# One small tile padded from 64 to 128 bytes, which shifts the on-chip address of every tile behind it

## The chip, the cores and the metric

The kernel runs on one core of one Trainium2 chip. The metric is the device time of one execution in microseconds (us). A core has five engines that run side by side: PE (TensorE, the matmuls; its weight loads are listed apart as PEld), DVE (VectorE), ACT (ScalarE), POOL (GpSimd) and SP (SyncE, which issues the DMAs here). The on-chip memory has 128 partitions; a tile is a rectangle of 128 partitions by some bytes, and its address is the byte within the partition at which it begins.

## The reference

One decoder block on `x` of 512 tokens by 1024 channels, all in float32:

```
h = RMSNorm(x);  [glu | q | k | v | g | gates] = h @ w_in
A: a = glu_a * sigmoid(glu_b) -> causal depthwise conv (31 taps) -> LayerNorm -> swish -> @ w_conv_proj
B: retention of 4 heads (rotary q, k; decay), norm per head, swish(g) gate -> @ w_ret_proj
x = x + (sigmoid(gA) * A + sigmoid(gB) * B) @ w_out
x = x + (silu(conv3(u1)) * conv3(u2)) @ w_down     with  [u1 | u2] = RMSNorm(x) @ w_up   (2 x 3072)
out = RMSNorm(x)
```

## The kernel before

Channels lie on the partitions and the 512 tokens along the free axis, so that an activation is a set of tiles of 128x512 float32 (2048 bytes in each partition). Every operand of a matmul is split in two rounded parts, high and low, and a product is made of three matmuls: high by high, high by low, low by high (L146 to L148 in `unit`). The part called lhsT is the stationary operand, loaded as a weight of 128x128; rhs is the moving operand, streamed column by column. In a row of the trace the moving tile stands first: `ps<-xg,whi` moves `xg` past the weights `whi`.

The weights come in one stream of 184 blocks of 128x1024 in the order of use. SP loads a block into `wraw` (3 buffers), ACT rounds it into `whi`, DVE subtracts to get `wlo` (3 buffers each, L92 to L108); this runs two blocks ahead of PE. The order of the work is fixed by the program: it is written out by hand, and a scheduler with priorities puts the long convolution on DVE (L337) behind everything else.

The stages, with the tile that moves through PE:

- Per head h = 0 to 3 (some 25 to 490 us): the projections of `h` move `xg`, the scaled input. `values` (L386) is the other way round: it moves the weights and loads `xg`. `scores` and `inner` (L416 to L455) move `A` (q, k, v), `sh` and `sl` (the scores), with 512, 384, 256 and 128 columns. `ret_proj` of the head before (L476) moves `R`.
- Gates and the last head's `ret_proj`, four times two units of `xg` and two of `R`; then the convolution's projection (L527), which moves `A` and `C` (high parts in `A`, low ones in `C`); then `w_out`, which moves `xg`.
- The feed-forward part: 48 units of `w_up` move `A`. `w_down` comes in two halves: each unit of the first moves eight `xg` tiles and four `R`, each of the second eight `xg` and four `C`. The last two units of the second half are cut in halves of 256 columns (L604 to L606) so that the final norm can begin.

Tiles of one tag lie together, and the tags follow each other in the order in which they are first used; each tile takes its own size, rounded up to 32 bytes. So the size of one tile sets the address of all tags that come after it. The tile concerned is `rtok` (L293): four float32 numbers per partition are used, the inverse norm of the tokens, written at L299 and read at L402; it is allocated as 16 numbers, 64 bytes.

Of the kernel before, what the change touches and what calls it, by code (L numbers as in the profile page):

```python
# [9 lines left out]
F32 = mybir.dt.float32  # L10
# [4 lines left out]
P = 128  # L15
# [6 lines left out]
NCH = S // P  # L22
# [25 lines left out]
def hybrid_block(  # L48
# [11 lines left out]
    sb = ctx.enter_context(tc.tile_pool(name="sb", bufs=1))  # L60
# [229 lines left out]
    with tc.high_priority(offset=-200):  # L290
        for i in range(KT):
            ss.add(xs[i])
    r_tok = sb.tile([P, 4 * NCH], F32, tag="rtok", name="rtok")[:, 0:NCH]  # L293
    rB = [None]
    cosr = sb.tile([P, S], F32, tag="cosr", name="cosr")
    sinr = sb.tile([P, S], F32, tag="sinr", name="sinr")
# [464 lines left out]
```

## Time and profile before

| | us |
|---|---|
| median of three runs (1089.64 to 1089.98) | 1089.82 |
| the profiled execution | 1090.43 |
| its span, first to last instruction | 1088.6 |
| PE busy | 1076.8 |
| DVE busy | 759.7 |
| ACT busy | 420.9 |

The profile is of one execution. Busy time of PE has overlaps in it, because each matmul begins before the one before it has ended: a matmul of 512 columns is listed with some 390 ns, but the next one begins about 227 ns after it. What counts for the time is this distance from start to start, called pitch below. It is read from the timeline as the difference of two start times, divided by the number of matmuls between them.

### The profile page before, as it was taken

To read this page: it belongs to the slowest core of one execution; us is meant where nothing else is said; L and a number is where in the kernel's file an instruction comes from. 1 tells how busy PE (TensorE), PEld (TensorE's weight loads), DVE (VectorE), ACT (ScalarE), POOL (GpSimd) and SP (SyncE) were. 2 spreads that over 40 slices of the span, in tenths; PEclk is the share of its full clock that TensorE was granted. 3 is DMA by queue.
4 is the path that set the end of the run, shared out by engine and by line. 5 is a ranking of instruction groups with operands and counts; after the bars stand their busy time and mean duration, and the time that the engine had idled before them with its cause. 6 is when DMAs were issued, how large, how long until landed. Compare 5 with 4: busy or idle time off the path is not lost.

```text
span 1088.6 us, 12567 instructions
## 1 busy us (share of the span) xinstructions
PE 1076.8 (99%) x4946; PEld 896.5 (82%) x4946; DVE 759.7 (70%) x1070; ACT 420.9 (39%) x555; POOL 20.0 (2%) x72
## 2 busy tenths in 40 slices
PE   8999999999999999999999999999999999999997
PEld 7888888888888888888888888888888888888886
DVE  5999699739996599937664555577777335767433
ACT  6343333434233331534462334444444113444331
POOL 1000000000000000000000000000000000000000
PEclk9999999999999999999999999999999999999999
DMA  7222132313222122222222432232222222222212
GB/s 273 97 97 87 59 97 97 101 64 97 96 97 88 58 97 97 80 76 78 97 97 97 145 126 97 78 110 95 93 95 95 96 96 97 97 97 97 97 58 78
DMA packets 32475, 105.48 MB, mean 97 GB/s; under 512 B 3616, under 2 KB 5920, under 8 KB 32416
## 3 DMA queue, kind: packets, MB, share of 16 engines
q1 hardware_dynamic: 32416, 104.69, 28.9%
q8 instruction: 38, 0.62, 0.2%
q14 instruction: 21, 0.17, 0.1%
HBM read 102.58 MB, written 2.10 MB: 96 GB/s over the span
## 4 chain that ended last, share of the span: by engine, by line
PE 97%; issue 1%; DVE 1%; DMA 0%; SPq 0%; ACT 0%; POOLq 0%; POOL 0%; DVEq 0%
PE ps L146 28%; PE ps L148 27%; PE ps L147 27%; PE ps L395 3%; PE ps L393 3%; PE ps L394 3%; PE ps L452 1%; PE ps L451 1%; PE ps L450 1%; PE ps L221 1%; PE ps L190 1%; PE ps L427 0%; PE ps L429 0%; PE ps L425 0%; DMA wraw<-in_wst_dram 0%
## 5 line engine op out<-in xcount | busy, mean ns | idle before, releaser
L105 ACT CAST whi<-wraw 128x1024 fp32r<-128x1024 f32 (+1 forms) x185 | 193.7, 1047 | 420.7 <-PE ps L147 282.5
L106 DVE TENSOR_TENSOR wlo<-wraw,whi 128x1024 fp32r<-128x1024 f32 (+1 forms) x185 | 224.8, 1216 | 69.4 <-ACT whi L105 66.5
L146 PE MATMUL ps<-xg,whi 128*128 128x512 f32 x672 | 263.4, 392 | 0.0
L148 PE MATMUL ps<-xg,wlo 128*128 128x512 f32 x672 | 261.9, 390 | 0.0
L147 PE MATMUL ps<-xg,whi 128*128 128x512 f32 x672 | 261.6, 389 | 0.0
L146 PE MATMUL ps<-A,whi 128*128 128x512 f32 x448 | 176.3, 393 | 0.0
L148 PE MATMUL ps<-A,wlo 128*128 128x512 f32 x448 | 174.8, 390 | 0.0
L337 DVE SCALAR_TENSOR_TENSOR C<-ap,par,C 128x512 f32<-128x512 f32 x240 | 166.1, 743 | 3.1 <-ACT C L334 2.7
L147 PE MATMUL ps<-A,whi 128*128 128x512 f32 x384 | 150.2, 391 | 0.0
L148 PEld LDWEIGHTS ps<-xg,wlo 128*128 128x128 f32 x672 | 126.1, 188 | 27.0
L147 PEld LDWEIGHTS ps<-xg,whi 128*128 128x128 f32 x672 | 126.2, 188 | 26.0
L146 PEld LDWEIGHTS ps<-xg,whi 128*128 128x128 f32 x672 | 126.2, 188 | 25.6
L148 PEld LDWEIGHTS ps<-A,wlo 128*128 128x128 f32 x448 | 84.1, 188 | 19.3
L146 PEld LDWEIGHTS ps<-A,whi 128*128 128x128 f32 x448 | 84.2, 188 | 18.0
L147 PEld LDWEIGHTS ps<-A,whi 128*128 128x128 f32 x384 | 72.2, 188 | 15.1
L308 DVE TENSOR_TENSOR t<-ps,rB 128x512 f32<-128x512 f32 x48 | 32.4, 686 | 72.2 <-PE ps L148 72.2
L558 DVE SCALAR_TENSOR_TENSOR t<-ap,par,t 128x512 f32<-128x512 f32 x96 | 71.5, 748 | 1.6
L182 DVE TENSOR_TENSOR x<-x,ps 128x512 f32<-128x512 f32 (+1 forms) x50 | 33.0, 664 | 53.9 <-PE ps L148 50.4
L552 DVE TENSOR_TENSOR ap<-ps,rB 128x512 f32<-128x512 f32 x48 | 32.9, 688 | 44.4 <-PE ps L148 44.4
L146 PE MATMUL ps<-R,whi 128*128 128x512 f32 x160 | 63.1, 395 | 0.0
L148 PE MATMUL ps<-R,wlo 128*128 128x512 f32 x160 | 62.7, 392 | 0.0
L147 PE MATMUL ps<-R,whi 128*128 128x512 f32 x160 | 62.2, 389 | 0.0
(135 smaller groups left out, 1180.6 us busy)
## 6 DMA issues: line engine op xcount, KB each, us to landing
wraw<-in_wst_dram SPq DMA_DIRECT2D x183, 512.0 KB, 3.3
x<-in_xT_dram SPq DMA_DIRECT2D x16, 256.0 KB, 2.8
out_dram<-t SPq DMA_DIRECT2D x8, 256.0 KB, 2.2
dec<-in_decay_dram SPq DMA_DIRECT2D x4, 256.0 KB, 2.6
t<-in_cs_dram SPq DMA_DIRECT2D x2, 256.0 KB, 4.2
wraw<-in_wst_dram SPq DMA_DIRECT2D x1, 384.0 KB, 4.8
par<-in_params_dram SPq DMA_DIRECT2D x1, 264.0 KB, 5.3
wraw<-in_wst_dram SPq DMA_DIRECT2D x1, 128.0 KB, 2.6
```

The costliest lines, as they stand in the source:

```text
L105: nc.scalar.copy(out=hi[:, sl], in_=raw[:, sl])
L106: nc.vector.tensor_tensor(out=lo[:, sl], in0=raw[:, sl], in1=f32(hi[:, sl]), op=ALU.subtract)
L146: nc.tensor.matmul(ps, lhsT=wh, rhs=xh, start=kt == 0, stop=False)
L147: nc.tensor.matmul(ps, lhsT=wh, rhs=xl, start=False, stop=False)
L148: nc.tensor.matmul(ps, lhsT=wl, rhs=xh, start=False, stop=kt == last)
L182: nc.vector.tensor_tensor(out=acc, in0=acc, in1=v, op=ALU.add)
L337: nc.vector.scalar_tensor_tensor(out=acc, in0=a[:, k:k + S], scalar=wcol(k), in1=acc, op0=ALU.mult, op1=ALU.add)
L393: nc.tensor.matmul(banks[c], lhsT=xh[:, sl], rhs=wh, start=kt == 0, stop=False)
L394: nc.tensor.matmul(banks[c], lhsT=xl[:, sl], rhs=wh, start=False, stop=False)
L395: nc.tensor.matmul(banks[c], lhsT=xh[:, sl], rhs=wl, start=False, stop=kt == KT - 1)
L552: nc.vector.tensor_tensor(out=u[:, FK - 1:], in0=ps, in1=rB[0], op=ALU.mult)
L558: nc.vector.scalar_tensor_tensor(out=c, in0=u[:, k:k + S], scalar=wcol(k), in1=c, op0=ALU.mult, op1=ALU.add)
```

## The change

`rtok` is allocated with 32 numbers (128 bytes) in place of 16 (64 bytes); the same four are used. No instruction is added, removed or moved: on every engine the same instructions stand in the same order. What differs is the address of the tags behind `rtok`, all 64 bytes further on.

```
-    r_tok = sb.tile([P, 4 * NCH], F32, tag="rtok", name="rtok")[:, 0:NCH]
+    r_tok = sb.tile([P, 8 * NCH], F32, tag="rtok", name="rtok")[:, 0:NCH]
```

First byte of a tag in the partition, from the program as built:

| tag (buffers x bytes) | before | after | before, past a multiple of 128 / 256 / 512 | after |
|---|---|---|---|---|
| x, wraw, xg, whi, wlo, ss, t | 19456 (x), 49152 (xg), 81920 (whi), 94208 (wlo) | the same | 0 / 0 / 0 | 0 / 0 / 0 |
| rtok | 126976 | 126976 | 0 / 0 / 0 | 0 / 0 / 0 |
| cosr, sinr (1 x 2048 each) | 127040, 129088 | 127104, 129152 | 64 / 64 / 64 | 0 / 128 / 128 |
| rB (1 x 2048) | 131264 | 131328 | 64 / 192 / 192 | 0 / 0 / 256 |
| ap (3 x 2168) | 133312 | 133376 | 64 (first) | 0 (first) |
| C (8 x 2048) | 139840 | 139904 | 64 / 64 / 64 | 0 / 128 / 128 |
| dec, A (1 and 16 x 2048) | 156224, 158272 | 156288, 158336 | 64 / 64 / 64 | 0 / 128 / 128 |
| sh, sl (5120 each) | 191296, 196416 | 191360, 196480 | 64 / 64 / 320 | 0 / 128 / 384 |
| G, nB, R (4, 1 and 8 x 2048) | 201536, 209728, 211776 | 201600, 209792, 211840 | 64 / 64 / 320 | 0 / 128 / 384 |

## Rows read from the trace of the kernel before

**Rows 1.** The page: busy time by engine, and the granted clock in 40 slices.
```profile
PE 1076.8 (99%) x4946; PEld 896.5 (82%) x4946; DVE 759.7 (70%) x1070; ACT 420.9 (39%) x555; POOL 20.0 (2%) x72
PEclk9999999999999999999999999999999999999999
```
**Rows 2.** The page: the chain that ended last, shares of the span by engine.
```profile
PE 97%; issue 1%; DVE 1%; DMA 0%; SPq 0%; ACT 0%; POOLq 0%; POOL 0%; DVEq 0%
```
**Rows 3.** All waits of PE: us in total, times, longest us.
```profile
PE ps L159 <- ACT xg L176: 1.7, 1, 1.7
...
PE ps L160 <- DVE xg L177: 0.9, 2, 0.6
```
**Rows 4.** The longest wait of ACT, same columns.
```profile
ACT whi L105 <- PE ps L147: 282.5, 127, 5.6
```
**Rows 5.** Timeline of PE, stage of w_out: start us, us listed, instruction.
```profile
642.25 0.39 PE L146 MATMUL ps<-xg,whi 128*128 128x512 f32 x1
...
676.25 0.39 PE L146 MATMUL ps<-xg,whi 128*128 128x512 f32 x1
```
**Rows 6.** Timeline of PE, stage of w_up.
```profile
760.45 0.39 PE L146 MATMUL ps<-A,whi 128*128 128x512 f32 x1
...
799.59 0.39 PE L146 MATMUL ps<-A,whi 128*128 128x512 f32 x1
```
**Rows 7.** Windows inside both: us, PE busy (count), granted clock, DMA share, GB/s.
```profile
642.30:676.30 34.00, 34.00 (x152) 1.00 0.27 93
760.50:799.50 39.00, 39.00 (x172) 1.00 0.29 95
```
**Rows 8.** Matmuls by moving tile, xg: count, duration in ns min/median/max, first and last start.
```profile
L146 PE MATMUL ps<-xg,whi x672: 387/389/486, 20.4 to 1059.3; 128*128 128x512 f32 x168
...
L393 PE MATMUL ps<-whi,xg x128: 389/389/398, 54.1 to 442.7; 128*128 128x512 f32 x128
```
**Rows 9.** The same for A (L148 has as many as L146).
```profile
L146 PE MATMUL ps<-A,whi x448: 392/394/477, 591.4 to 1009.8; 128*128 128x512 f32 x150
...
L147 PE MATMUL ps<-A,whi x384: 388/394/398, 679.2 to 1010.0; 128*128 128x512 f32 x192
```
**Rows 10.** The same for R (L147 and L148 have as many).
```profile
L146 PE MATMUL ps<-R,whi x160: 392/394/443, 154.6 to 899.9; 128*128 128x512 f32 x160
```
**Rows 11.** The same for C (L148 has as many as L146).
```profile
L147 PE MATMUL ps<-C,whi x88: 388/388/397, 591.7 to 1054.0; 128*128 128x512 f32 x88
...
L146 PE MATMUL ps<-C,whi x24: 394/394/398, 1010.5 to 1053.8; 128*128 128x512 f32 x24
```
**Rows 12.** Timeline of PE, one unit of w_down, from R to xg and back.
```profile
867.59 0.40 PE L146 MATMUL ps<-xg,whi 128*128 128x512 f32 x1
...
869.90 0.39 PE L147 MATMUL ps<-xg,whi 128*128 128x512 f32 x1
...
873.08 0.40 PE L146 MATMUL ps<-R,whi 128*128 128x512 f32 x1
...
873.78 0.39 PE L146 MATMUL ps<-R,whi 128*128 128x512 f32 x1
```
**Rows 13.** Timeline of PE, head 0, from a projection into values.
```profile
53.43 0.39 PE L146 MATMUL ps<-xg,whi 128*128 128x512 f32 x1
...
54.11 0.39 PE L393 MATMUL ps<-whi,xg 128*128 128x512 f32 x1
...
54.79 0.39 PE L393 MATMUL ps<-whi,xg 128*128 128x512 f32 x1
```
**Rows 14.** Groups by line, shapes apart: 256 columns, C and xg (x, busy us, mean ns).
```profile
L605 PE MATMUL ps<-xg,whi 128*128 128x256 f32 x32 | 9.1, 283 | 0.0
...
L605 PE MATMUL ps<-C,whi 128*128 128x256 f32 x16 | 4.5, 279 | 0.0
```
**Rows 15.** Groups by line: DVE's subtraction into xg and into A.
```profile
L170 DVE TENSOR_TENSOR xg<-t,xg 128x512 fp32r<-128x512 f32 x24 | 16.5, 689 | 9.6 <-ACT xg L169 9.6
...
L170 DVE TENSOR_TENSOR A<-t,A 128x512 fp32r<-128x512 f32 x16 | 10.9, 682 | 0.0
```

## The prediction

> **What bounds the kernel now.** [...] The waits of PE come third, to see whether PE ever stands still for somebody: the longest of its five is 1.7 us, the shortest 0.9 us, and their lines (L159 to L161, L253, L221, L190) are those of the first 20 us and of the end [rows 3]. In between it goes from matmul to matmul without a pause. So no wait can be removed here, and no engine beside PE can give time back; what is left is how long one matmul keeps the next one back.
>
> That is not in the durations but in the start times, and there the trace shows two levels. In the stage of w_out, which moves `xg`, the start goes from 642.25 to 676.25 us [rows 5]. The window between holds 152 matmuls [rows 7], of which two had begun before it, so the pitch is 34.00 us / 150 = 226.7 ns. In the stage of w_up, which moves `A`, it is 760.45 to 799.59 us [rows 6] over 172 less the one that lies before the first row [rows 7]: 39.14 us / 171 = 228.9 ns. Same shape, same weights buffers, same clock, similar DMA share (0.27 and 0.29). The listed medians split in the same way: 389 ns for L146 with `xg` and for L393, which moves `whi` [rows 8], 394 ns for L146 with `A`, `R` or `C` [rows 9 to 11]. The split follows the address: `xg`, `whi` and `wlo` begin at multiples of 128 bytes, `A`, `R`, `C`, `sh` and `sl` 64 bytes past one. It doesn't follow the buffer's tag (three tags are slow alike), or the stage (w_down has both in one unit).
>
> **What the change costs and gives.** It adds and removes no instruction, and the queues keep their order, so there is no wait to be added and none to be removed. It moves the five slow tags to multiples of 128 bytes. If these set the pitch, they fall to the pitch of `xg`.
>
> First term, the steady pitch. Moving operands of 512 columns from moved tiles: 448 + 448 + 384 of `A` [rows 9], 3 x 160 of `R` [rows 10], 88 + 24 + 24 of `C` [rows 11], 1896 in all. Each is worth 228.9 - 226.7 = 2.2 ns, which is 4.2 us. Scores and inner have 18 more per head of 512 columns from `A`, `sh` and `sl` (6 and 12), 72 in all: 0.16 us.
>
> Second term, the passage between the two levels. In w_down a unit goes from `R` to `xg` and back. The first ten matmuls after the passage into `xg` take 867.59 to 869.90 us, 2.31 us where ten steady ones take 2.27: some 0.045 us lost [rows 12]. The first three after the passage into `R` take 0.70 us where three steady ones take 0.687: some 0.015 us [rows 12]. By the order of the units there are 22 passages of the first kind (3 after `ret_proj`, 4 in the gates, 1 into w_out, 8 and 6 in w_down) and as many of the second. That makes 1.0 + 0.3 = 1.3 us. It goes only if the passage between addresses is its cause and not the change of tile as such. The trace says the former: from a projection into `values`, where the moving tile changes from `xg` to `whi` and both lie on multiples of 128, three matmuls take 0.68 us before and 0.68 us behind the border [rows 13], with nothing lost.
>
> Third, the shapes that have no clean pair of rows. At 256 columns L605 is listed with 283 ns from `xg` and with 279 ns from `C` [rows 14], so the sign may turn there: 48 matmuls of the last units may lose up to 4 ns each, 0.2 us. Of the 216 narrower ones in scores and inner I know only that the wide ones differ by 2.2 ns; either way that is at most 0.5 us. I take zero for both and keep -0.5 to +0.7 us for the range.
>
> Fourth, the other engines. DVE and ACT read and write the moved tiles too. DVE's subtraction takes 689 ns into `xg` and 682 ns into `A` [rows 15], the slower one on the multiple of 128; so moving `A` may lengthen such an operation by 7 ns or shorten it. On some 600 DVE operations on moved tiles that is 4 us of 759.7 us busy, and PE is the cover: what DVE and ACT owe PE is the next weights, and ACT's longest wait is for PE to give back a `whi` buffer, 282.5 us over 127 times [rows 4], so the weights are there long before PE wants them. If this cover were gone, those 4 us would be the price. I take nothing. The DMA into a moved tile (`dec`, four times) is far ahead of its use: nothing.
>
> The sum is 4.2 + 0.2 + 1.3 = 5.7 us. The profiled execution took 1090.43 us, 1.8 us outside its span; less 5.7 that is 1084.7 us. The median of the runs is 0.6 us below the profiled one, so I forecast 1084.1 us for a median. It goes faster by 0.5%, and PE stays the bound; no other wait comes late next.
>
> [...]
>
> **The rivals.**
> No change, 1089.8 us: the offset within 128 bytes isn't what counts. Two readings of the table of addresses allow it. All slow tags lie above byte 127,000 and all fast ones below 107,000, and the change moves none across; or the step that counts is 256 bytes or more, and the moved tiles still stand 128 past a multiple of 256, while every fast one stands on a multiple of 2048. The trace can't separate these from my reading. For it: nothing that moves through PE lies high and on a multiple of 128. [...]
>
> Slower, about 1095.5 us: the excess grows with the distance from a multiple of 256. Then 64 bytes cost 2.2 ns, 128 bytes cost 4.4, and the first two terms come once more on top: 1089.8 + 5.7. [...] Against it: `R` stands 320 past a multiple of 512 and `A` 64, and both have 394 ns in L146 [rows 9, 10], so at least by 512 distance doesn't count. It decides if L146 with `A` goes above 394 ns.
>
> Half of it, 1085.5 to 1088.8 us: only the steady term goes and the passages stay (1089.8 - 4.4 = 1085.4), or only those tiles gain that also changed their place to 256 in a favourable way, or the narrow shapes lose the 0.7 us. Against it stand the rows of the border without loss.
>
> **How the numbers follow.** The forecast has 0.70, the half case 0.08, no change 0.12, slower 0.10. The forecast's own range is 1083.0 to 1085.3: the third item's bounds and half a us for the passages, of which I saw one unit. To leave out no more than 2 in 10 the range has to take in the half case and come to the edge of no change: 1082.8 to 1089.9. What a measurement can tell from no change is about 0.2%, 2.2 us. Faster by more than that is the forecast and three quarters of the half case, 0.76; the rest of it and no change make 0.14; slower 0.10.
>
> **What would show it.** In the profile after, L146 with `A`, `R` and `C` should be listed with 389 ns in place of 394, the pitch in w_up should be 226.7 ns, and a unit of w_down should go from `R` to `xg` with no step in its pitch. The stages of w_up and w_down are then shorter by about 2.6 and 1.2 us, w_out lasts as long as before. I am wrong if the medians of `A` stay at 392 to 394 ns (place or a wider step), if they rise (distance), or if they fall and PE then shows waits for `wlo` or `whi` between 100 and 1050 us, which would mean that the other engines had been just in time.

## The result and the profile after

The changed kernel takes 1096.49 us (median of six runs, 1095.78 to 1096.72), the kernel before in the same runs 1089.75 us: a ratio of 1.0059, 95% interval 1.0048 to 1.0070. It is slower by 6.7 us, where 5.7 us faster was forecast. The profiled execution has a span of 1094.7 us, 6.1 us more than before.

The page of the kernel after, the rows that answer to [rows 1, 2]: PE is the bound as before, at the same granted clock (1.00 in the stretches shown below and in those of [rows 7]), and it is PE that is busy for longer.

```profile
PE 1083.8 (99%) x4946; PEld 897.4 (82%) x4946; DVE 760.1 (69%) x1070; ACT 419.7 (38%) x555; POOL 19.4 (2%) x72
PEclk9999999999999999999999999999999999999998
...
PE 97%; issue 1%; DVE 1%; DMA 0%; SPq 0%; ACT 0%; POOLq 0%; POOL 0%; DVEq 0%
```

All of PE's waits in the kernel after; the columns are total us, times and longest us, as in [rows 3].

```profile
PE ps L221 <- DVE tokr L214: 1.2, 1, 1.2
PE ps L253 <- POOL neghalf L248: 1.0, 1, 1.0
PE ps L190 <- ACT t L612: 1.0, 1, 1.0
PE ps L160 <- DVE xg L177: 0.9, 2, 0.6
PE ps L159 <- ACT xg L176: 0.8, 1, 0.8
```

No wait has come. The one of 1.7 us in the first 20 us is even 0.9 us shorter (0.8 us), at the first matmuls, which wait for the first tiles; its cause is open. So the time is in the pitch, and the timeline shows where. First the stage of w_out and the stage of w_up in the kernel after, first and last start, with the windows that count the matmuls between; they answer to [rows 5 to 7].

```profile
642.15 0.39 PE L146 MATMUL ps<-xg,whi 128*128 128x512 f32 x1
...
676.15 0.39 PE L146 MATMUL ps<-xg,whi 128*128 128x512 f32 x1
...
760.13 0.39 PE L146 MATMUL ps<-A,whi 128*128 128x512 f32 x1
...
799.17 0.39 PE L146 MATMUL ps<-A,whi 128*128 128x512 f32 x1
```

```profile
642.20:676.10 33.90, 33.90 (x151) 1.00 0.30 98
760.20:799.10 38.90, 38.90 (x169) 1.00 0.28 95
```

`xg`, which wasn't moved, needs 34.00 us for 150 matmuls, the same 226.7 ns as before. `A` needs 39.04 us for 168: 232.4 ns, where it had 228.9. `R`, in the `ret_proj` of head 0, went from 228.9 to 233.4 ns. Before:

```profile
156.66 0.39 PE L146 MATMUL ps<-R,whi 128*128 128x512 f32 x1
...
175.20 0.39 PE L146 MATMUL ps<-R,whi 128*128 128x512 f32 x1
```

After:

```profile
156.55 0.40 PE L146 MATMUL ps<-R,whi 128*128 128x512 f32 x1
...
175.46 0.39 PE L146 MATMUL ps<-R,whi 128*128 128x512 f32 x1
```

That is 18.54 us before and 18.91 us after, each over 81 matmuls. Where the 6.1 us lie can be counted: both kernels have the same matmuls in the same order, so the change of every distance from start to start can be added up by moving tile. `A` in w_up has 4.5 us more over 1152 matmuls (3.9 ns each, a little above the stretch shown), `R` 1.7 us over 480, `A` and `C` in the convolution's projection 0.9 us over 192, and `C` in w_down 0.2 us. Two things go the other way. The matmuls that move `xg` take 0.6 us less behind the first 20 us, which fits the passages: the one from `R` into `xg` that took 2.31 us for ten matmuls [rows 12] takes 871.22 to 873.50 us, 2.28, some 0.03 us less at 22 places. The first 20 us take 0.8 us less, most of it the shorter wait. 4.5 + 1.7 + 0.9 + 0.2 - 0.6 - 0.8 = 5.9 us; the remaining 0.2 us are spread over the rest. The 288 matmuls of scores and inner, where the moving tile and the weights (cut from `A`) both moved by 64 bytes, changed by less than 0.1 us in all.

The median of one line is a poor gauge for this. For L146 with `A` it went from 394 [rows 9] down to 393 ns while the pitch rose by 3.5 ns:

```profile
L146 PE MATMUL ps<-A,whi x448: 390/393/478, 591.9 to 1015.5; 128*128 128x512 f32 x150
```

The reason is that before, the three matmuls of a triple were not alike. In the `ret_proj` of head 0 the distances to the next start are 232, 226 and 229 ns in turn at L146, L147 and L148 (listed with 394, 388 and 392 ns); in the stretch of w_up of [rows 6] they are 229, 232 and 226. So 228.9 ns is the mean of a turn of three, and the long place isn't bound to one line. With the mean over the three lines the listed durations do follow the pitch: `A` had 393, 391 and 390 ns and has 395 at all three. L147 with `R`, before and after (busy us, mean ns):

```profile
L147 PE MATMUL ps<-R,whi 128*128 128x512 f32 x160 | 62.2, 389 | 0.0
...
L147 PE MATMUL ps<-R,whi 128*128 128x512 f32 x160 | 63.1, 394 | 0.0
```

### The profile page after: what moved, and what is told of

It is laid out like the page before. It is cut to its first block, busy times and chain, and to the rows that moved or that the text cites. A ratio compares the mean times of both kernels' runs of the same rounds, so it can differ in the third digit from the quotient of the medians.

```text
span 1094.7 us, 12567 instructions
## 1 busy us (share of the span) xinstructions
PE 1083.8 (99%) x4946; PEld 897.4 (82%) x4946; DVE 760.1 (69%) x1070; ACT 419.7 (38%) x555; POOL 19.4 (2%) x72
## 4 chain that ended last, share of the span: by engine, by line
PE 97%; issue 1%; DVE 1%; DMA 0%; SPq 0%; ACT 0%; POOLq 0%; POOL 0%; DVEq 0%
PE ps L146 28%; PE ps L147 27%; PE ps L148 27%; PE ps L395 3%; PE ps L393 3%; PE ps L394 3%; PE ps L451 1%; PE ps L452 1%; PE ps L450 1%; PE ps L221 1%; PE ps L190 1%; PE ps L427 0%; PE ps L429 0%; PE ps L425 0%; DMA wraw<-in_wst_dram 0%
## 5 line engine op out<-in xcount | busy, mean ns | idle before, releaser
L146 PE MATMUL ps<-xg,whi 128*128 128x512 f32 x672 | 262.9, 391 | 0.0
L148 PE MATMUL ps<-xg,wlo 128*128 128x512 f32 x672 | 261.7, 389 | 0.0
L147 PE MATMUL ps<-xg,whi 128*128 128x512 f32 x672 | 261.7, 389 | 0.0
L146 PE MATMUL ps<-A,whi 128*128 128x512 f32 x448 | 177.0, 395 | 0.0
L148 PE MATMUL ps<-A,wlo 128*128 128x512 f32 x448 | 176.9, 395 | 0.0
L147 PE MATMUL ps<-A,whi 128*128 128x512 f32 x384 | 151.6, 395 | 0.0
L148 PEld LDWEIGHTS ps<-xg,wlo 128*128 128x128 f32 x672 | 126.1, 188 | 26.5
L146 PEld LDWEIGHTS ps<-xg,whi 128*128 128x128 f32 x672 | 126.2, 188 | 25.9
L147 PEld LDWEIGHTS ps<-xg,whi 128*128 128x128 f32 x672 | 126.2, 188 | 25.7
L148 PEld LDWEIGHTS ps<-A,wlo 128*128 128x128 f32 x448 | 84.2, 188 | 20.1
L146 PEld LDWEIGHTS ps<-A,whi 128*128 128x128 f32 x448 | 84.2, 188 | 20.1
L147 PEld LDWEIGHTS ps<-A,whi 128*128 128x128 f32 x384 | 72.2, 188 | 17.0
L148 PE MATMUL ps<-R,wlo 128*128 128x512 f32 x160 | 63.2, 395 | 0.0
L146 PE MATMUL ps<-R,whi 128*128 128x512 f32 x160 | 63.2, 395 | 0.0
L147 PE MATMUL ps<-R,whi 128*128 128x512 f32 x160 | 63.1, 394 | 0.0
```

What stands on the lines that cost most here:

```text
L146: nc.tensor.matmul(ps, lhsT=wh, rhs=xh, start=kt == 0, stop=False)
L147: nc.tensor.matmul(ps, lhsT=wh, rhs=xl, start=False, stop=False)
L148: nc.tensor.matmul(ps, lhsT=wl, rhs=xh, start=False, stop=kt == last)
```

## The experiments

All are edits of the kernel before and leave the computation whole. The first four ask what it is in the address that counts: the place, the remainder of the moving tile alone, or the moving tile and the weights together. Every pitch is taken as above, between two starts in one stage.

**pad256: multiples of 256.**

```
-    r_tok = sb.tile([P, 4 * NCH], ...)
+    r_tok = sb.tile([P, 16 * NCH], ...)
```

Expected: 

> rtok takes 256 bytes, so that A, C, sh, sl and R begin at multiples of 256 (A 256 past a multiple of 512, R on one). Theory D (the pitch follows the moving tile's distance from a multiple of 256): pitch of A and R falls to 226.7 ns, no step at the passages, 1083 to 1084.5 us. Theory P (the place, above byte 127,000, and some other property of the address): no fall, pitch 229 ns or more, 1089 us or more. Theory B (only multiples of 512 or 2048 are good): R better than A, or neither, 1088 us or more.

Measured: 1084.02 us (1083.65 to 1084.87), ratio 0.9944 (0.9929 to 0.9958): faster than both kernels. The timeline of w_up, and w_down where `R` gives way to `xg`:

```profile
760.10 0.39 PE L146 MATMUL ps<-A,whi 128*128 128x512 f32 x1
...
799.54 0.39 PE L146 MATMUL ps<-A,whi 128*128 128x512 f32 x1
...
863.24 0.39 PE L148 MATMUL ps<-R,wlo 128*128 128x512 f32 x1
863.46 0.39 PE L146 MATMUL ps<-xg,whi 128*128 128x512 f32 x1
...
864.14 0.39 PE L146 MATMUL ps<-xg,whi 128*128 128x512 f32 x1
```

`A` needs 39.44 us for 174 matmuls, 226.7 ns, and three matmuls after the passage take 0.68 us, as three steady ones do: no step is left. So the place above byte 127,000 is no cause, and `A` at 256 past a multiple of 512 does as well as `R` on one, which needs 18.36 us for 81 matmuls, 226.7 ns too:

```profile
156.94 0.39 PE L146 MATMUL ps<-R,whi 128*128 128x512 f32 x1
...
175.30 0.39 PE L146 MATMUL ps<-R,whi 128*128 128x512 f32 x1
```

**pad192: the other side of 128.**

```
-    r_tok = sb.tile([P, 4 * NCH], ...)
+    r_tok = sb.tile([P, 12 * NCH], ...)
```

Expected: 

> rtok takes 192 bytes: the moved tiles lie 192 past a multiple of 256, 64 past a multiple of 128 as in the kernel before. Theory D in its growing form (2.2 ns at 64, 5.8 to 6.8 at 128, more at 192): pitch 236 to 239 ns, about 1100 to 1105 us. Theory D in a form with the distance to the nearest multiple: pitch 229 ns as before, 1089.8 us. Theory of the prediction (only the remainder by 128 counts, already shaken): 229 ns.

Measured: 1098.21 us, ratio 1.0073 (1.0056 to 1.0089). `A` starts at 760.61 and 165 matmuls later at 799.11:

```profile
760.61 0.40 PE L146 MATMUL ps<-A,whi 128*128 128x512 f32 x1
...
799.11 0.39 PE L146 MATMUL ps<-A,whi 128*128 128x512 f32 x1
```

That is 233.3 ns. Not the 229 ns that the same remainder by 128, or the distance to the nearest multiple, would give, and less than the growing form had asked for.

**all64: the weights and xg shifted with the rest.**

```
-    identr = sb.tile([P, P], F32R, tag="identr", name="identr")
+    identr = sb.tile([P, P + 16], F32R, tag="identr", name="identr")[:, 0:P]
```

Expected: 

> identr is 64 bytes wider, so that xg, whi and wlo too move by 64 bytes, and A, C, sh, sl, R come to 128 past a multiple of 256, as in the changed kernel. Theory D, absolute address of the moving tile: xg rises to 228.9 ns, A and R stay at 232 to 234 ns, about 1096.5 plus 2400 x 2.2 ns = 1101 us. Theory L (only the difference between moving tile and weights counts): xg stays at 226.7, A and R at 228.9 ns, 1089.8 us.

Measured: 1090.44 us, ratio 1.0004 (0.9995 to 1.0013). Every tile behind `identr`, and so every operand of these matmuls, stands 64 bytes further on than before, and no pitch has changed:

```profile
642.35 0.39 PE L146 MATMUL ps<-xg,whi 128*128 128x512 f32 x1
...
675.67 0.39 PE L146 MATMUL ps<-xg,whi 128*128 128x512 f32 x1
...
760.56 0.39 PE L146 MATMUL ps<-A,whi 128*128 128x512 f32 x1
...
799.70 0.39 PE L146 MATMUL ps<-A,whi 128*128 128x512 f32 x1
```

`xg` at 64 past a multiple of 128 has 33.32 us / 147 = 226.7 ns, and `A`, at the very addresses that it has in the changed kernel, 39.14 us / 171 = 228.9 ns. The absolute address is out; what is left is the difference between moving tile and weights.

**w128: the weights moved away from xg.**

```
+        if i == 0:
+            gap = sb.tile([P, 32], F32, tag="gap", name="gap")
+            nc.gpsimd.memset(gap, 0.0)
         if i in (0, 3):
             split_half(emitted[0])
...
-    r_tok = sb.tile([P, 4 * NCH], ...)
+    r_tok = sb.tile([P, 12 * NCH], ...)
```

Expected: 

> A gap of 128 bytes between xg and whi, and rtok of 192 bytes: xg stays on a multiple of 2048, the weights lie 128 past a multiple of 256, A, C, sh, sl and R 64 past a multiple of 256 as before. Theory D, absolute address of the moving tile: xg 226.7 and A, R 228.9 ns as before; only the weights that move in values (384 matmuls) go to 232 to 233 ns; 1091 to 1092.5 us. Theory L (difference to the weights): xg lies 128 from the weights by 256 and goes to 232 to 233 ns, 1100 us or more. A third, that the stationary operand's address counts by itself: every unit's pitch rises, the A and xg ones alike.

Measured: 1110.71 us, ratio 1.0187 (1.0172 to 1.0203), the slowest of all. `xg`, on a multiple of 2048 as always, goes from 650.27 to 684.43 us in 147 matmuls, 232.4 ns:

```profile
650.27 0.39 PE L146 MATMUL ps<-xg,whi 128*128 128x512 f32 x1
...
684.43 0.39 PE L146 MATMUL ps<-xg,whi 128*128 128x512 f32 x1
```

`A`, 64 past a multiple of 256 as in the kernel before but now 192 past the weights, has 233.3 ns (38.50 us for 165 matmuls from 765.26 us on), the pitch of pad192. Both pitches rose, so the third form, that the weights' address counts by itself, is still open here.

**w128_r256: the changed kernel's remainder with the weights on the same.** As w128, with `rtok` of 256 bytes.

Expected: 

> A, C, sh, sl and R begin 128 past a multiple of 256, as in the changed kernel, but the weights too (gap of 128 bytes between xg and whi); xg stays on a multiple of 256. Theory L (what counts is moving minus stationary address, by 256): A and R fall to 226.7 ns at the very remainder that made them slow in the changed kernel; xg, 128 off the weights, rises to 232.6 ns and the weights that move past xg in values to 233. That is 1083.9 + about 2016 x 5.9 + 384 x 6.4 ns = 1098 to 1099 us. Theory D (absolute remainder of the moving tile): A and R at 232 to 233 ns, xg at 226.7, about 1097 to 1099 us as well, so the pitches tell and not the time.

Measured: 1099.19 us, ratio 1.0082 (1.0067 to 1.0097).

```profile
650.70 0.39 PE L146 MATMUL ps<-xg,whi 128*128 128x512 f32 x1
...
685.00 0.40 PE L146 MATMUL ps<-xg,whi 128*128 128x512 f32 x1
...
770.63 0.39 PE L146 MATMUL ps<-A,whi 128*128 128x512 f32 x1
...
808.71 0.39 PE L146 MATMUL ps<-A,whi 128*128 128x512 f32 x1
```

`A` needs 38.08 us for 168 matmuls, 226.7 ns, at 128 past a multiple of 256, where the changed kernel has it at 232.4; `xg` needs 34.30 us for 147, 233.3 ns. The times of the two theories were alike, the pitches are not: the difference decides. The third form of w128 ends here too: the weights stand 128 past a multiple of 256, and `A` is fast.

**wlo128: only the low weights off.** A gap of 128 bytes between `whi` and `wlo`, `rtok` of 128 bytes. The lines behind the edit stand 3 lower: L149 to L151 are L146 to L148 of before, L397 and L398 are L394 and L395.

```
+        if h == 0:
+            gap = sb.tile([P, 32], F32, tag="gap", name="gap")
+            nc.gpsimd.memset(gap, 0.0)
         lo = sb.tile([P, HS], F32R, tag="wlo", bufs=3, name=nm("wlo"))
...
-    r_tok = sb.tile([P, 4 * NCH], ...)
+    r_tok = sb.tile([P, 32], ...)
```

Expected: 

> A gap of 128 bytes between whi and wlo: whi, xg, A, C, sh, sl, R stand on multiples of 256, wlo alone 128 past one. One matmul in three then has its stationary tile 128 off the moving one. Theory L with the weights of the matmul itself: L148 is long, a third of the full excess, mean pitch about 228.6 ns, 1083.9 + 4300/3 x 5.9 ns = 1092 us or so. Theory L with the weights that are loaded while the matmul runs, those of the next one: the same mean, but L147 (before L148) is the long one. If only equal remainders in all three lock the fast pitch: 232 ns or more everywhere, 1108 us.

Measured: 1102.93 us, ratio 1.0116 (1.0099 to 1.0133), 11 us more than the first two cases gave and 5 less than the third. By tile, durations min/median/max in ns:

```profile
L149 PE MATMUL ps<-A,whi x448: 389/389/485, 598.6 to 1021.2; 128*128 128x512 f32 x150
L151 PE MATMUL ps<-A,wlo x448: 393/397/404, 599.0 to 1021.7; 128*128 128x512 f32 x150
L150 PE MATMUL ps<-A,whi x384: 392/396/398, 687.5 to 1021.5; 128*128 128x512 f32 x192
...
L397 PE MATMUL ps<-whi,xg x128: 389/389/389, 54.7 to 448.1; 128*128 128x512 f32 x128
...
L398 PE MATMUL ps<-wlo,xg x128: 395/395/395, 54.9 to 448.3; 128*128 128x512 f32 x128
```

From start to start the three lines with `A` have 226.9, 232.5 and 234.1 ns; from 759.86 us on, 165 matmuls take 38.13 us, 231.1 ns each. Neither of my two forms is right alone: both L151, which uses `wlo`, and L150, while which `wlo` is loaded (with `xg` the last load for L151 starts at 1071.4 us, as the last L150 does), are long; the one that has nothing to do with it is not. In `values`, where `wlo` moves, only its own matmul is long. All of it agrees with one reading: a matmul is held up if the tile that it moves differs by 256 either from its own weights or from those loaded meanwhile. It is a reading of this run; no other run has the two halves of the weights apart.

**off32_96 and off160_224: the distances between.** `rtok` of 32 or 160 bytes, and the tile before `R` 64 bytes longer.

```
-        b = t512(tag, bufs)
+        b = (sb.tile([P, S + 16], F32, tag=tag, bufs=bufs, name=nm(tag))[:, 0:S]
+             if tag == "nB" else t512(tag, bufs))
...
-    r_tok = sb.tile([P, 4 * NCH], ...)
+    r_tok = sb.tile([P, 8], ...)       # off160_224: [P, 40]
```

Expected: 

> rtok takes 32 bytes and the tile before R 64 more: A, C, sh, sl stand 32 past the weights by 256, R 96 past. [...] If the excess goes in steps of 64 bytes: A at 226.7 or 228.9, R at 228.9 or 233.

> A, C, sh, sl stand 160 past the weights by 256, R 224 past. [...] Below 226.7 ns nowhere; if R is faster than that, there is a better offset than zero.

Measured: 1099.01 us, ratio 1.0081 (1.0061 to 1.0101), and 1099.69 us, ratio 1.0087 (1.0067 to 1.0107). The rows of off32_96, `R` over 81 matmuls and `A` over 162:

```profile
157.76 0.39 PE L146 MATMUL ps<-R,whi 128*128 128x512 f32 x1
...
176.66 0.39 PE L146 MATMUL ps<-R,whi 128*128 128x512 f32 x1
...
760.70 0.39 PE L146 MATMUL ps<-A,whi 128*128 128x512 f32 x1
...
798.50 0.39 PE L146 MATMUL ps<-A,whi 128*128 128x512 f32 x1
```

And of off160_224 `R` over 81, `A` over 165:

```profile
157.62 0.40 PE L146 MATMUL ps<-R,whi 128*128 128x512 f32 x1
...
176.52 0.40 PE L146 MATMUL ps<-R,whi 128*128 128x512 f32 x1
...
760.07 0.40 PE L146 MATMUL ps<-A,whi 128*128 128x512 f32 x1
...
798.73 0.40 PE L146 MATMUL ps<-A,whi 128*128 128x512 f32 x1
```

The form of steps falls: 32 bytes have 233.3 ns, more than the 228.9 of 64, so the excess doesn't go in steps of 64. At 160 and 224 no pitch is below 226.7 ns, as expected, and `R` at 224, 32 short of the next multiple of 256, still has 233.3. Moving tile minus weights, by 256, against the pitch:

| bytes | 0 | 32 | 64 | 96 | 128 | 160 | 192 | 224 |
|---|---|---|---|---|---|---|---|---|
| ns | 226.7 | 233.3 | 228.9 | 233.3 | 232.4 to 233.4 | 234.3 | 233.3 | 233.3 |

Every distance tried but 0 costs 5.7 to 7.6 ns per matmul, save 64, which costs 2.2 on average over its turn of three.

**c128: one moving tile in three off.** `rtok` of 128 bytes, `dec` 128 bytes longer, so that of the moving tiles `C` alone keeps the changed kernel's addresses.

```
-        dec = t512("dec", 1)
+        dec = sb.tile([P, S + 32], F32, tag="dec", name=nm("dec"))[:, 0:S]
...
-    r_tok = sb.tile([P, 4 * NCH], ...)
+    r_tok = sb.tile([P, 8 * NCH], ...)
```

Expected: 

> rtok of 128 bytes as in the changed kernel, and 128 bytes more behind dec: A, sh, sl and R stand on multiples of 256 like the weights, C alone 128 past one. In the projection of the convolution the moving tiles of a triple are A, C, A past whi, whi, wlo: one moving tile in three is off. Theory L, a matmul is long by about 7 ns when its moving tile's remainder by 256 differs from that of its own weights or of the weights loaded while it runs: L147 alone is long there (234 ns, the two others 226 to 227, mean 229), in w_down every matmul from C is at 232 to 234 ns, everything else at 226.7; about 1084 + 64 x 7 ns + 72 x 6.5 ns = 1085 us. If one unequal tile upsets the whole triple, as the unequal wlo upset two of three: L147 and L148 long, mean 231, 1085.5 us. Theory D (absolute address): the same as L here, since the weights are on multiples of 256.

Measured: 1085.18 us, ratio 0.9954 (0.9937 to 0.9971). The projection of the convolution, whose triples move `A`, `C`, `A`:

```profile
601.95 0.39 PE L146 MATMUL ps<-A,whi 128*128 128x512 f32 x1
...
603.32 0.39 PE L146 MATMUL ps<-A,whi 128*128 128x512 f32 x1
...
L147 PE MATMUL ps<-C,whi x88: 387/395/398, 589.8 to 1048.9; 128*128 128x512 f32 x88
...
L146 PE MATMUL ps<-A,whi x448: 389/389/486, 589.6 to 1004.6; 128*128 128x512 f32 x150
...
L148 PE MATMUL ps<-A,wlo x448: 388/389/397, 590.1 to 1005.1; 128*128 128x512 f32 x150
```

Two triples take 1.37 us, some 229 ns a matmul; over the whole stage it is 228.9 ns. The long one is that from `C`: to the next start it takes 234.3 ns on average over the 64 triples, the two others 226.7 and 225.7. The time and the place are those of theory L (and of theory D, which forecasts the same here). The reading found with wlo128 had been set down before the run, and it held for the moving tile; c128 can't test its part on the weights.

## Why the prediction was wrong

Right were the bound (PE's pitch, no wait before or after), the reading of two levels of pitch from the trace, and even the sum: the gain of 5.7 us worked out from `xg`'s pitch is there, 6.1 us by the ratio's middle, but in pad256 and not in this kernel. The passages between the levels are an effect of unequal addresses as I had argued from [rows 13]; in pad256 they are gone (0.68 us for three matmuls).

The step that failed is the condition of the first term: "It moves the five slow tags to multiples of 128 bytes. If these set the pitch, they fall to the pitch of `xg`." They don't set it. In the kernel before, two classes of tiles differ in their remainder by 128, and I took the coarsest step that separates them. The same rows would bear a remainder by 256, and also a difference to the weights, since the tiles of the weights begin on multiples of 2048 and their blocks are cut from them in steps of 512; the rival "no change" named the first, nobody the second. What the runs show is the second: all64 shifts everything and nothing happens, w128_r256 makes `A` fast at the addresses that the change gave it, by moving the weights. The change brings the difference from 64 bytes (228.9 ns), of the distances tried the one cheap one besides zero, to 128 (232.4 and 233.4 ns), one of the dear ones.

The rival that came out at the right time, "slower, about 1095.5 us" by a cost that grows with the distance, was right in its place, the moved tiles, and in its sum by chance: it asked 4.4 ns per matmul and doubled passages, and the runs show 5.7 to 6.7 ns and cheaper passages (2.28 us for ten matmuls in place of 2.31). It went by the moving tile's own address, which all64 rules out, and by a cost that grows, where 32 bytes cost more than 64. Its mark, a median above 394 ns at L146 with `A`, did not appear either (393), because L146 had already been listed with 392 or 394 ns before, the middle and the long place of the turn of three.

Three readings beside it were wrong as well. The split of the listed medians, 389 against 394 ns, goes by L146 alone: L147 with `C` stood at 388 [rows 11], and with `R` too. By these medians the prediction's own sign would have read "place or a wider step", no change, where the pitch had risen. The 0.16 us of scores and inner, and the term kept for their narrower shapes, had no ground: there both operands moved together, their difference by 256 is 0 in both kernels, and in pad256 these 288 matmuls gave back 0.1 us. And the five waits are at L159, L160, L190, L221 and L253; L161 has none.

Open are three things: whether what differs counts against the matmul's own weights or the next ones' load (wlo128 has both long, c128 can't tell them), why 64 bytes ahead (228.9 ns) costs a third of what 64 behind does (233.3 ns at 192) and comes in turns of three, and distances that are no multiple of 32, which weren't tried.

## What to carry to other kernels

Where matmuls follow each other without a pause, compare the pitch of tiles in different places, from start times over whole triples and not from the median of one line; a difference of 2 ns was worth 6 us here. If the tiles differ in address, ask what the address is measured against before you pad: here it was the other operand, and moving and stationary tiles that begin at the same remainder by 256 had 226.7 ns, against 228.9 to 234.3 at the seven other distances tried. Before a step of alignment is taken from two classes of tiles, list every rule that separates them; a shift of all tiles together, and one of the other operand alone, told them apart here.

## What the runs showed of the hardware that was not expected

- The pitch of 128x512 matmuls with a fresh weight load each is 226.7 ns when moving tile and weights have the same remainder by 256 bytes, and 228.9 to 234.3 ns for the other multiples of 32. At 64 the 228.9 ns are a mean: from start to start it is 229, 232 and 226 ns in turn (w_up of the kernel before).
- What the equal remainder is made no difference in the runs: 226.7 ns at 0 (`A` in pad256), at 64 (`xg` in all64) and at 128 (`A` in w128_r256). Nor did it matter whether a tile lies low or high in the partition: 226.7 ns in pad256 for `xg` at 49152 and for `R` at 211968.
- One tile off didn't hold up the whole triple. With one moving tile off (c128) its own matmul had 234.3 ns and the two others 226.7 and 225.7, mean 228.9; with one weight tile off (wlo128) two of three were long, 232.5 and 234.1 ns, and the third had 226.9, mean 231.1.
